# Scaling tokens by two expert weights: the first output tile stored in two transfers of 1 and 11 tokens, and the last tile's weights moved behind the second input tile

## The chip, the core and the metric

The kernel runs on one core of one Trainium2 chip. The metric is the device time of one execution in microseconds; each time given for a kernel is the median of several runs, and one further execution was taken with the hardware profiler. Of the core's engines two compute here: the vector engine (DVE) and the scalar engine (ACT). The sync engine (SP) only issues transfers. All transfers, whichever engine issued them, are carried by the core's 16 DMA engines; the transfers of SP stand in one queue and those of ACT in another.

## The reference: what is computed

Every token is a row of 512 float32 numbers. Each token has two weights, and the output holds the token twice, once times each weight. The expert indices are an input, but nothing is computed from them.

```python
# x (16, 1024, 512) f32, expert_weights (16, 1024, 2) f32
x_expanded = x[:, :, np.newaxis, :].repeat(k, axis=2)     # k = 2
weights = expert_weights[..., np.newaxis]
return (x_expanded * weights).astype(np.float32)          # (16, 1024, 2, 512)
```

So 33.55 MB of tokens and 0.13 MB of weights are read, and 67.11 MB are written.

## The kernel before, in words

**Tiles.** The 16384 tokens are 128 per "token slot" (one in each of the 128 partitions), 128 slots in all. `groups` (line 32) cuts them into six input tiles of 24, 24, 24, 24, 24 and 8 slots; below, "token" means such a slot, as in the title. Within a tile a partition holds consecutive tokens, so that an input tile of 24 is one run of 48 KB in each partition (6144 KB in all). An output tile holds 12 tokens with both copies, which is again 48 KB in each partition; so an input tile gives two output tiles, and the last gives one of 8 tokens. There are 11 output tiles. I number input tiles x0 to x5 and output tiles out0 to out10.

**Buffers.** All weights have one buffer of their own (`w_tile`). Input tiles have two buffers in turn, output tiles two.

**Weights.** SP issues three transfers ahead of everything else: the weights of x0 (line 53, 24 KB, in pieces of 192 bytes), those of x1 to x4 (line 54, 96 KB, in 512 pieces of 192 bytes) and those of x5 (line 58, 8 KB, in 128 pieces of 64 bytes). I call them w0, w-middle and w-last.

**Loads.** `load(i)` (line 74) issues the input tile's transfer on ACT's queue: x0 in six parts of 4 tokens (1024 KB each, 8 KB per partition), every other tile in one. x0 and x1 are issued at the start (line 88), x2 after the instructions of tile 0, and so on (line 119), since the buffer has to be free.

**Compute.** For each token and each of the two weights one multiplication of 128x512 is done, with the weight as a scalar per partition. Counting weights through the whole input as `c`, every third one (`c % 3 == 2`) goes to ACT (line 100) and the two others to DVE (line 106). The first token of x0 has c = 0 and 1, and so both its multiplications are DVE's.

**Stores.** When 12 tokens of an output tile (or the tile's last) are done, SP issues its store (line 115).

**What sets the order.** Each engine works through its own list of instructions in program order; waits between engines are put in by the framework from the tiles' overlaps. A transfer also signals completion on one of eight semaphores, given out in turn; when a semaphore comes round again, the new transfer's issue waits until the earlier transfer on it has landed. In the program before, for instance, the sixth part of x0 waits for w0, and x1 waits for the first part of x0, and out0 waits for w-middle besides its multiplications. Such a wait holds up everything behind it in that engine's list.

Of the kernel before, what the change touches and what calls it, by code (L numbers as in the profile page):

```python
# [1 line left out]

# [4 lines left out]


@with_exitstack
def kernel(  # L10
    ctx: ExitStack,
    tc: tile.TileContext,
    x: bass.AP,
    expert_indices: bass.AP,
    expert_weights: bass.AP,
    out: bass.AP,
):
    nc = tc.nc

    batch, seq, hidden = x.shape  # L20
    k = expert_weights.shape[-1]
    P = nc.NUM_PARTITIONS
    ntok = batch * seq
    assert ntok % P == 0
    A_TOTAL = ntok // P

    f32 = mybir.dt.float32
    row = k * hidden
    TX = 24
    TO = 12  # L30

    groups = [[24], [24], [24], [24], [24], [8]]
    assert sum(sum(g) for g in groups) == A_TOTAL

    xf = x.rearrange("b s h -> (b s) h")
    of = out.rearrange("b s k h -> (b s) (k h)")
    wf = expert_weights.rearrange("b s k -> (b s) k")

    w_pool = ctx.enter_context(tc.tile_pool(name="w_pool", bufs=1))
    x_pool = ctx.enter_context(tc.tile_pool(name="x_pool", bufs=2))  # L40
    o_pool = ctx.enter_context(tc.tile_pool(name="o_pool", bufs=2))

    w_tile = w_pool.tile([P, A_TOTAL * k], f32)

    def rows(of_all, done, T):
        return of_all[done * P : (done + T) * P, :].rearrange(
            "(p a) n -> p (a n)", a=T
        )

    T0 = sum(groups[0])  # L50
    G = len([g for g in groups[1:] if sum(g) == T0])
    head = (1 + G) * T0
    nc.sync.dma_start(out=w_tile[:, : T0 * k], in_=rows(wf, 0, T0))
    nc.sync.dma_start(
        out=w_tile[:, T0 * k : head * k].rearrange("p (g n) -> p g n", g=G),
        in_=wf[T0 * P : head * P, :].rearrange("(g p a) n -> p g (a n)", g=G, p=P),
    )
    nc.sync.dma_start(
        out=w_tile[:, head * k :], in_=rows(wf, head, A_TOTAL - head)
    )  # L60

    tiles = []
    done = 0
    for group in groups:
        T = sum(group)
        a0 = 0
        for n in group:
            tiles.append((done, T, a0, n))
            a0 += n
        done += T  # L70

    loaded = []

    def load(i):
        if i >= len(tiles):
            return
        done, T, a0, n = tiles[i]
        x_tile = x_pool.tile([P, TX * hidden], f32)
        src = rows(xf, done, T)
        step = TX // 6 if i == 0 else n  # L80
        for at in range(0, n, step):
            nc.scalar.dma_start(
                out=x_tile[:, at * hidden : (at + step) * hidden],
                in_=src[:, (a0 + at) * hidden : (a0 + at + step) * hidden],
            )
        loaded.append(x_tile)

    for i in range(2):
        load(i)
    for i, (done, T, a0, n) in enumerate(tiles):  # L90
        x_tile = loaded[i]
        outr = rows(of, done, T)
        for t in range(n):
            if t % TO == 0:
                o_tile = o_pool.tile([P, TO * row], f32)
            for kk in range(k):
                c = (done + a0 + t) * k + kk
                o = t % TO * row + kk * hidden
                if c % 3 == 2:
                    nc.scalar.mul(  # L100
                        out=o_tile[:, o : o + hidden],
                        in_=x_tile[:, t * hidden : (t + 1) * hidden],
                        mul=w_tile[:, c : c + 1],
                    )
                    continue
                nc.vector.tensor_scalar(  # L106
                    out=o_tile[:, o : o + hidden],
                    in0=x_tile[:, t * hidden : (t + 1) * hidden],
                    scalar1=w_tile[:, c : c + 1],
                    scalar2=None,  # L110
                    op0=mybir.AluOpType.mult,
                )
            if (t + 1) % TO == 0 or t + 1 == n:
                at = t // TO * TO
                nc.sync.dma_start(  # L115
                    out=outr[:, (a0 + at) * row : (a0 + t + 1) * row],
                    in_=o_tile[:, : (t + 1 - at) * row],
                )
        load(i + 2)

# [1 line left out]
_INS = ['x', 'expert_indices', 'expert_weights']  # L122
_OUTS = [((16, 1024, 2, 512), 'float32')]


# [23 lines left out]
```

## Time and profile before

| | |
|---|---|
| median of 3 runs | 240.72 us (240.66 to 240.78) |
| profiled execution, its own time | 240.62 us |
| its span, first to last instruction | 238.9 us |
| moved by DMA in the span | 100.81 MB, mean 422 GB/s |
| DVE busy | 69.0 us (29%), 171 multiplications |
| ACT busy | 54.9 us (23%), 85 multiplications and one table load |
| queue of SP (weights and stores) | 2400 packets, 67.24 MB |
| queue of ACT (token loads) | 1584 packets, 33.56 MB |

The profile's page cuts the span into 40 slices of 5.97 us and gives for each the busy tenths of the engines, the mean busy share of the 16 DMA engines, and the GB/s moved. A window view does the same for stretches that one chooses. In both a packet counts, with all its bytes, where it starts; a packet of 48 KB is long (some 1.8 us on its DMA engine), so that the rate in a stretch of a few us can go up and down without any real change. The chain of waits follows the last instruction back to what released it. The list of transfers gives the time from the issue of each to its landing, which holds the time that it stood in the queue.

### The profile page before, as it was taken

How to read it: one execution, taken by the hardware profiler on the slowest of the kernel's cores; microseconds unless marked ns; L12 is line 12 of the kernel's file. 1: busy time of each engine (PE TensorE's matmuls, PEld its weight loads, DVE VectorE, ACT ScalarE, POOL GpSimd, SP SyncE). 2: the span in 40 equal slices, each digit the busy share in tenths (PEclk: the TensorE clock that was granted, in tenths of full speed). 3: DMA queues.
4: the chain of work that ended last, by engine and by line, in shares of the span. 5: the costliest groups of instructions: out<-in, count | busy, mean ns of one | idle time of the engine just before them, and what ended most of it. 6: DMA issues, size and time to landing. Idle time of an engine off the chain costs nothing.

```text
span 238.9 us, 364 instructions
## 1 busy us (share of the span) xinstructions
DVE 69.0 (29%) x171; ACT 54.9 (23%) x86; POOL 0.2 (0%) x4
## 2 busy tenths in 40 slices
DVE  0890300004609100190063037003706406415000
ACT  0870300004308000170071034003406106213000
POOL 0000000000000000000000000000000000000000
DMA  6999999999999999999999999999989899999994
GB/s 244 420 443 395 495 395 395 494 428 395 428 494 395 413 494 411 395 446 469 403 411 502 395 420 453 436 411 428 469 379 496 381 428 469 436 411 428 436 439 197
DMA packets 3986, 100.81 MB, mean 422 GB/s; under 512 B 1168, under 2 KB 1168, under 8 KB 1168
## 3 DMA queue, kind: packets, MB, share of 16 engines
q1 hardware_dynamic: 2400, 67.24, 65.2%
q10 hardware_dynamic: 1584, 33.56, 33.1%
q14 instruction: 2, 0.02, 0.0%
HBM read 33.69 MB, written 67.11 MB: 422 GB/s over the span
## 4 chain that ended last, share of the span: by engine, by line
DMA 66%; DVE 13%; another core or an unknown queue 11%; issue 0%; DVEq 0%; SPq 0%
DMA out_dram<-o_tile 54%; DVE o_tile L106 13%; DMA x_tile<-in_x_dram 11%; DVEq L144 0%; DVEq L106 0%; SPq L115 0%
## 5 line engine op out<-in xcount | busy, mean ns | idle before, releaser
L106 DVE TENSOR_SCALAR o_tile<-x_tile,w_tile 128x512 f32<-128x512 f32 x171 | 69.0, 480 | 149.3 <-DMA out_dram<-o_tile 105.3
L100 ACT ACTIVATE o_tile<-x_tile,w_tile 128x512 f32<-128x512 f32 x85 | 53.6, 709 | 155.5 <-DMA out_dram<-o_tile 116.8
L100 ACT ACT_TABLE_LOAD x1 | 1.3, 1283 | 6.7 <-DMA x_tile<-in_x_dram 6.7
L133 POOL MEMSET const-bfloat16-1.0<- 128x1 bf16 x1 | 0.1, 101 | 0.0
L133 POOL MEMSET const-uint8-127<- 128x1 uint8 x1 | 0.1, 101 | 0.0
L133 POOL MEMSET const-float32-0.0<- 128x1 f32 x1 | 0.1, 98 | 0.2 <-issue 0.2
L133 POOL MEMSET const-float32-1.0<- 128x1 f32 x1 | 0.1, 98 | 0.0
## 6 DMA issues: line engine op xcount, KB each, us to landing
out_dram<-o_tile SPq DMA_DIRECT2D x10, 6144.0 KB, 33.6
x_tile<-in_x_dram ACTq DMA_DIRECT2D x4, 6144.0 KB, 43.9
x_tile<-in_x_dram ACTq DMA_DIRECT2D x6, 1024.0 KB, 10.6
out_dram<-o_tile SPq DMA_DIRECT2D x1, 4096.0 KB, 19.5
x_tile<-in_x_dram ACTq DMA_DIRECT2D x1, 2048.0 KB, 24.0
w_tile<-in_expert_weights_dram SPq DMA_DIRECT2D x1, 96.0 KB, 11.1
w_tile<-in_expert_weights_dram SPq DMA_DIRECT2D x1, 24.0 KB, 2.9
w_tile<-in_expert_weights_dram SPq DMA_DIRECT2D x1, 8.0 KB, 13.2
```

The source lines that it names most:

```text
L100: nc.scalar.mul(out=o_tile[:, o : o + hidden], in_=x_tile[:, t * hidden : (t + 1) * hidden], mul=w_tile[:, c : c + 1],)
L106: nc.vector.tensor_scalar(out=o_tile[:, o : o + hidden], in0=x_tile[:, t * hidden : (t + 1) * hidden], scalar1=w_tile[:, c : c + 1], scala ...
L133: nc = _bacc.Bacc("TRN2", target_bir_lowering=False, num_devices=1)
```

## The change

The order in which the transfers are written down changes, and one store becomes two.

- The weights of the last tile (8 KB) are no longer issued by SP as its third transfer, but by ACT, after x0 and x1, so they stand behind x1 in the queue of loads.
- w-middle is written down after the load of x0; it is still SP's second transfer.
- `cuts` names token 1 as a cut of the first tile, so out0 is stored in two transfers: the first token (512 KB, 4 KB per partition), issued as soon as its two multiplications are done, and the other 11 (5632 KB, 44 KB per partition).

```diff
-    nc.sync.dma_start(out=w_tile[:, : T0 * k], in_=rows(wf, 0, T0))
-    nc.sync.dma_start(
-        out=w_tile[:, T0 * k : head * k].rearrange("p (g n) -> p g n", g=G),
-        in_=wf[T0 * P : head * P, :].rearrange("(g p a) n -> p g (a n)", g=G, p=P),
-    )
-    nc.sync.dma_start(
-        out=w_tile[:, head * k :], in_=rows(wf, head, A_TOTAL - head)
-    )
...
-    for i in range(2):
-        load(i)
+    nc.sync.dma_start(out=w_tile[:, : T0 * k], in_=rows(wf, 0, T0))
+    load(0)
+    nc.sync.dma_start(
+        out=w_tile[:, T0 * k : head * k].rearrange("p (g n) -> p g n", g=G),
+        in_=wf[T0 * P : head * P, :].rearrange("(g p a) n -> p g (a n)", g=G, p=P),
+    )
+    load(1)
+    nc.scalar.dma_start(
+        out=w_tile[:, head * k :], in_=rows(wf, head, A_TOTAL - head)
+    )
+    cuts = [[1]] + [[]] * (len(tiles) - 1)
...
-            if (t + 1) % TO == 0 or t + 1 == n:
-                at = t // TO * TO
+            at = t // TO * TO
+            if t + 1 in cuts[i] or (t + 1) % TO == 0 or t + 1 == n:
+                lo = max([c for c in cuts[i] if c <= t] + [at])
                 nc.sync.dma_start(
-                    out=outr[:, (a0 + at) * row : (a0 + t + 1) * row],
-                    in_=o_tile[:, : (t + 1 - at) * row],
+                    out=outr[:, (a0 + lo) * row : (a0 + t + 1) * row],
+                    in_=o_tile[:, (lo - at) * row : (t + 1 - at) * row],
                 )
```

The semaphores are given out in turn, so the change also moves some of the waits that come from reuse. In the changed program's list ACT issues the six parts of x0, then x1, then w-last, and only then comes its table load and its first multiplication; w-last has the semaphore of w-middle, and its issue waits until w-middle has landed. The first part of the store waits for DVE alone. The second part waits for DVE, for ACT, and for the second part of x0. x2 now waits for the first part of the store where it waited for w-last.

## The prediction

> **What bounds the kernel now.** I read the page's slices first, then the windows, then the chain of waits, then the list of transfers with the starts of the single engines. The slices:
>
> ```profile
> DVE  0890300004609100190063037003706406415000
> ACT  0870300004308000170071034003406106213000
> DMA  6999999999999999999999999999989899999994
> GB/s 244 420 443 395 495 395 395 494 428 395 428 494 395 413 494 411 395 446 469 403 411 502 395 420 453 436 411 428 469 379 496 381 428 469 436 411 428 436 439 197
> ```
>
> The computing engines are idle most of the time, the DMA row is at 9 from the second slice to the last but one, but for two 8s that packets counted at their start explain (the windows below show no loss there). So the kernel is bound by its bytes, and a change can only act where the DMA engines are not full or not at their full rate. The windows (columns: stretch, its length, DVE, ACT, POOL busy with counts, clock, DMA share, GB/s) find those places:
>
> ```profile
> 0.00:2.00 2.00, 0.00 (x0) 0.00 (x0) 0.20 (x4) 1.00 0.19 29
> 2.00:4.00 2.00, 0.00 (x0) 0.00 (x0) 0.00 (x0) 1.00 0.81 299
> 4.00:14.00 10.00, 6.82 (x17) 6.61 (x10) 0.00 (x0) 1.00 1.03 417
> 15.50:16.50 1.00, 0.98 (x3) 0.23 (x1) 0.00 (x0) 1.00 1.07 320
> 16.50:16.90 0.40, 0.40 (x2) 0.40 (x2) 0.00 (x0) 1.00 0.89 225
> 30.00:110.00 80.00, 19.41 (x49) 15.04 (x25) 0.00 (x0) 1.00 1.00 433
> 110.00:220.00 110.00, 36.56 (x91) 28.22 (x45) 0.00 (x0) 1.00 1.00 432
> 236.00:239.00 3.00, 0.00 (x0) 0.00 (x0) 0.00 (x0) 1.00 0.03 11
> ```
>
> From 30 to 220 us the rate is 433 and 432 GB/s, whether loads and stores are mixed or stores run alone. All 100.81 MB at 433 take 232.8 us, so the span of 238.9 holds 6.1 us that are not full rate. I put a price on each place as its length times (1 - rate/433): start 0 to 2 us, 1.9; ramp 2 to 4 us, 0.6; the parts of x0 with the weights between them, 4 to 14 us, 0.4; the dip at 15.5 to 16.9 us, 0.26 + 0.19 = 0.45. That leaves 2.8 us for the end, where the 16 engines finish one after the other and the last signal travels (the last row). The dip lies about two us after out0's store is issued, which is the first store of all:
>
> ```profile
> 13.38 17.16 SPq L115 DMA_DIRECT2D out_dram<-o_tile  x2
> ```
>
> I read the dip as the price of the first stores joining a stream of loads; by 18.7 us the mix runs at its usual rate. A packet counts where it starts, so 0.45 is rough.
>
> The opening as it is issued and as it lands:
>
> ```profile
> 0.73 5.94 ACTq L82 DMA_DIRECT2D x_tile<-in_x_dram  x7
> 5.85 2.46 DVE L106 TENSOR_SCALAR o_tile<-x_tile,w_tile 128x512 f32<-128x512 f32 x6 [5.85 <-DMA x_tile<-in_x_dram]
> 6.70 1.28 ACT L100 ACT_TABLE_LOAD   x1 [6.70 <-DMA x_tile<-in_x_dram]
> 7.99 5.18 ACT L100 ACTIVATE o_tile<-x_tile,w_tile 128x512 f32<-128x512 f32 x8
> ```
>
> ```profile
> w_tile<-in_expert_weights_dram SPq DMA_DIRECT2D x1, 96.0 KB, 11.1
> w_tile<-in_expert_weights_dram SPq DMA_DIRECT2D x1, 24.0 KB, 2.9
> w_tile<-in_expert_weights_dram SPq DMA_DIRECT2D x1, 8.0 KB, 13.2
> ```
>
> The chain of waits says that later on stores follow stores: after each store's landing DVE does 16 multiplications in 6.44 us and the next store is issued, while the other one is still in the queue (6.29 MB at 433 GB/s is 14.5 us even when alone). So the store queue doesn't run dry.
>
> **The change part by part.**
>
> *w-last leaves SP.* w-middle is issued at 1.16 us and lands 11.1 us later, at 12.3: its small pieces go in turn with the 8 KB packets of x0. Before, w-last came behind it (1.63 + 13.2 = 14.8 us). In SP's queue its place is free now.
>
> *w-last in ACT's list.* Its issue waits for w-middle. ACT is in order, so the table load and all of ACT's multiplications wait with it: the table load moves from 6.7 to 12.3 + 0.5 (w-last's issue, the duration that SP showed) = 12.8 us, the first multiplication to 14.1, and the eighth ends at 14.1 + 8 x 0.707 = 19.7 us, where it ended at 13.2. DVE doesn't wait for ACT, and its buffers for out0 and out1 are both free at first. Queued behind ACT are the second part of the store, SP's, and x2, ACT's. The second part is issued at 19.7 us in place of 13.4, which is 6.3 us later. ACT's other eight multiplications of tile 0 are now held by ACT alone: 19.7 + 8 x 0.707 = 25.4 us, where before the last part of x0 let them start only at 28.07 and they ended at 30.1. So out1 and x2 are issued near 25.5, some 4.7 us earlier than 30.2.
>
> On the path this costs nothing as long as the DMA engines have other bytes. They have: x0 and x1 are 2 x 6.29 MB and the first token 0.52 MB, 13.1 MB, which at 417 to 433 GB/s keep them full until about 33 us. If x1 had not been issued at 5.85 us, the 6.3 us would show in full. Then out0's second part and x1 go in turn, out1 is behind in the queue from 25.5 us, and x1 lands earlier than the 57.05 us at which DVE now waits for it. No engine's lateness reaches the store queue after that, by the 14.5 against 6.44 us above. I cost it at 0.
>
> *The first token's store.* DVE's two multiplications end at 5.85 + 2 x 0.48 = 6.8 us. The transfer is issued then, but it stands in SP's queue behind w-middle's pieces, so its bytes move at about 12 us, not at 7. It is 0.52 MB, 1.2 us of all engines, taken from x0: the last parts of x0 come about that much later, and against the present trace the last part is still earlier, since no 48 KB store packets stand between its 8 KB packets until 20 us.
>
> *One more transfer.* It adds 0.33 us on SP's queue, which waits 212 us in all, and 9 more packets on each DMA engine (8 data, 1 signal). Priced by the 0.4 us of 4 to 14 us and the 878 packets under 512 B that start before 14 us, 55 per engine: 0.4 / 55 = 0.007 us each, 0.06 us. w-last's pieces leave that stretch, the same 9 packets, for one where the small price may vanish: between -0.06 and 0. The two together: 0, within 0.06.
>
> The Trainium skill (DMA: Bandwidth & Descriptors, "Anatomy of one DMA" and "Rules for kernel authors") speaks against the cut: it gives each DMA a fixed cost of about 2 us, fitted on another issue path, and wants 1 MiB or more. By that rule, laid end to end, the extra store would make the sum 242.7 us. This trace shows the six 1024 KB parts of x0 following each other in 4 to 14 us at 417 GB/s, so a fixed cost per transfer is hidden while others are queued.
>
> *The joining of stores.* This is the only place where I see a price that changes. Before: one joining, 0.45 us. After: two. The first, at about 12 us, is of 4 KB packets; it ends at about 16 us, and the stores stop. The second, at about 21 us, is of 44 KB packets amid x1's 48 KB loads. Neither is in the trace. For each the lower bound is 0: from 30 us on large loads and stores go in turn without loss, and loads that join running stores show none. The upper bound is the dip, 0.45. So the sum of both is 0 to 0.9 against 0.45, a change of -0.45 to +0.45. I take 0.2 for the first (only 32 KB per DMA engine in all, less to fill the way with) and 0.45 for the second (its packets and its quiet store queue are nearest to the dip's row): +0.2.
>
> *The end.* The last store's size and the last stages are as before. Which of the 16 engines is last can shift; I take 0, within 0.3 of a 2.8 us end.
>
> Sum: 0 + 0 + 0.2 + 0 = +0.2 us. On the profiled execution, 238.9 + 1.7 outside the span = 240.62, that is 240.8; the median of the runs is 0.1 above the profiled execution, so 240.9.
>
> **The rivals.**
>
> *Two full joinings (slower).* If the way has to be filled anew after the stores' pause and small packets cost as much as large ones, the change is +0.45; with the end shifted by up to 0.3 it is 241.2 to 241.5. For it: the dip is there at all, and the stores do pause from about 16 to 21 us. Against it: the dip was seen once, with 8 KB loads.
>
> *Cheaper joining (faster, the other side).* If the small store opens the way under the cover of the 8 KB loads and the large one then joins free like the later mixes, the dip goes: -0.45, with w-last's -0.06 about 240.2. It decides at a saving over 0.48 us, so it needs nearly all of the dip and something of the opening or the end.
>
> *ACT's wait reaches the end (slower).* The 6.3 us in full make 247.0. For it: ACT does stand still until 12.3 us. Against it: 13.1 MB of queued bytes cover 12 us beyond that point. It would need a store queue that runs dry afterwards, and none of the windows from 30 to 220 us shows that.
>
> *The cut doesn't do what it says.* The first token is behind w-middle, so the early store is not early; then the change is nothing but ACT's delay, covered: 240.7. That is inside the forecast's range.
>
> **How the numbers follow.** A difference of 0.2%, 0.48 us, is about what a measurement of this kernel can tell from no change. The forecast with the ineffective cut has 0.53, of which 0.03 crosses the upper bound; two full joinings 0.27, three in ten of it within the bound; the wait reaching the end, in whole or part, 0.04; the cheaper joining 0.16, of which I leave 0.14 beyond the bound. Faster 0.14, slower 0.03 + 0.19 + 0.04 = 0.26, and what is left, 0.60, the same. The range: from 240.72 - 0.45 - 0.06 = 240.2 to 240.72 + 0.45 + 0.06 + 0.3 = 241.5; outside of it are the wait and the tips, under 2 in 10.
>
> **What would show it.** In the changed profile w-middle lands near 12.3 us, ACT's table load starts near 12.8, the second part is issued near 19.7, out1 and x2 near 25.5, and the DMA row stays at 8 or 9 from the second slice on. A window with a reduced rate near 12 to 13 us and another near 20 to 22 tell the joinings: none, one or two. The windows from 50 to 220 us stay at 432 to 433. The prediction is wrong if a slice in the middle is under 8, if the steady rate is another, or if the opening loses a microsecond more or less than here.

## The result: half a per cent slower, and the profile after

The changed kernel's median is 241.93 us (240.82 to 243.43, 21 runs), that of the kernel before in the same comparison 240.72 us (240.55 to 241.4, 21 runs): 1.0051 of the time, with a 95% interval of 1.0041 to 1.0061. That is 1.2 us slower, above the range of 240.2 to 241.5. The spread has grown as well, from 0.85 to 2.6 us. The profiled execution took 241.6 us with a span of 239.8; before it was 240.62 with 238.9.

The slices of the changed kernel's page, as shown of before:

```profile
DMA  7999998999999999999999999999999999999894
GB/s 252 395 417 479 379 503 375 483 410 394 508 410 395 402 492 418 402 460 426 418 451 443 410 443 435 426 410 459 435 404 456 418 465 435 402 443 451 388 437 186
```

Still no slice in the middle is under 8: no stretch went empty. The windows (the same columns as before: stretch, length, DVE, ACT, POOL, clock, DMA share, GB/s):

```profile
4.00:14.00 10.00, 6.60 (x16) 0.81 (x1) 0.00 (x0) 1.00 1.01 397
14.00:30.00 16.00, 6.61 (x16) 10.38 (x17) 0.00 (x0) 1.00 1.02 428
30.00:60.00 30.00, 6.42 (x16) 5.01 (x8) 0.00 (x0) 1.00 1.00 433
60.00:80.00 20.00, 6.42 (x16) 5.02 (x8) 0.00 (x0) 1.00 1.02 433
110.00:220.00 110.00, 36.58 (x91) 28.22 (x45) 0.00 (x0) 1.00 1.00 432
236.00:240.00 4.00, 0.00 (x0) 0.00 (x0) 0.00 (x0) 1.00 0.08 33
```

Two rows of the kernel before beside them:

```profile
14.00:30.00 16.00, 6.25 (x16) 5.00 (x8) 0.00 (x0) 1.00 1.08 444
236.00:240.00 4.00, 0.00 (x0) 0.00 (x0) 0.00 (x0) 1.00 0.03 10
```

The last row is the plainest difference: before, 10 GB/s were left after 236 us, now 33. The window counts a packet where it starts, and that is too coarse for less than a microsecond (it makes 14 to 30 us look slower than before, 428 against 444). So I spread each packet's bytes evenly over its own duration, from the trace's packet records, and took what is missing against 433.3 GB/s:

```
                               before    after
lost up to 40 us                3.78      3.74
lost from 40 to 220 us          0.05      0.59   (0.31 of it in 60 to 80 us)
lost from 220 us to the last
  packet's end                  1.15      1.27
last packet's end             237.64    238.24
from there to the end of span   1.30      1.56
```

The changes add up to -0.04 + 0.54 + 0.12 + 0.26 = 0.88 us, the difference of the two spans. The opening, where the prediction looked, costs nothing more. The loss comes in small pieces later and at the end. The 16 engines' last packets end, before, at 235.8 to 236.7 us on 13 engines and at 237.0, 237.2 and 237.6 on three; after, at 236.2 to 237.1 on 12 engines and at 237.6, 238.1, 238.1 and 238.2 on four.

The opening after the change (timeline rows of the changed kernel: start, duration, engine, line, operation, count, and the wait before it):

```profile
12.82 0.33 ACTq L87 DMA_DIRECT2D w_tile<-in_expert_weights_dram  x1
13.19 1.28 ACT L101 ACT_TABLE_LOAD   x1 [13.19 <-DMA w_tile<-in_expert_weights_dram]
14.48 9.91 ACT L101 ACTIVATE o_tile<-x_tile,w_tile 128x512 f32<-128x512 f32 x16
24.42 0.37 ACTq L74 DMA_DIRECT2D x_tile<-in_x_dram  x1
48.42 5.01 ACT L101 ACTIVATE o_tile<-x_tile,w_tile 128x512 f32<-128x512 f32 x8 [24.03 <-DMA out_dram<-o_tile]
```

ACT stands still until w-middle has landed at 12.8 us, its sixteen multiplications run through without a gap, and x2 is issued at 24.4. The second part of out0 is issued at 19.51 us. At 48.42 ACT waits for a store and no longer for x1, as foretold. The changed kernel's list of transfers (KB, and us from issue to landing):

```profile
out_dram<-o_tile SPq DMA_DIRECT2D x1, 5632.0 KB, 28.8
out_dram<-o_tile SPq DMA_DIRECT2D x1, 512.0 KB, 9.9
w_tile<-in_expert_weights_dram ACTq DMA_DIRECT2D x1, 8.0 KB, 48.2
```

The first token's store, issued at 6.6, lands at 16.5, behind w-middle as said. The last row I had not foreseen. w-last, 8 KB, issued at 12.82, lands at 61 us, and that is not only the wait behind x1, whose packets end at 44.6. Packets by queue in 46 to 60 us (q1: SP's stores, q10: ACT's loads; count, MB, share of 16 engines), first of before:

```profile
q1 hardware_dynamic: 66, 3.24, 53.5%
q10 hardware_dynamic: 67, 2.51, 41.5%
```

and of the changed kernel:

```profile
q1 hardware_dynamic: 133, 5.73, 94.5%
q10 hardware_dynamic: 133, 0.01, 0.6%
```

For 14 us the load queue carries nothing but w-last: 124 packets of 64 bytes and 9 signals of 4 bytes. The store queue has as many packets in that time, 117 of 44 or 48 KB and 16 signals. So each engine takes one packet from each queue in turn, and each 64-byte packet costs the load queue a 48 KB store packet's time. An engine has eight data packets of w-last, 8 x 1.815 = 14.5 us. All that time x2 stands behind them, and its first packets start at about 60 us. I call this the hold. The Trainium skill (DMA: Bandwidth & Descriptors, "Queues, rings and completion order") says that an engine goes round its queues packet by packet, with some 9 to 17 descriptors to a typical packet. The turns here agree, 133 against 133, but not that size: each 64-byte piece took a turn of its own.

### The profile page after: what moved, and what is told of

It is laid out like the page before. It is cut to its first block, busy times and chain, and to the rows that moved or that the text cites. A ratio compares the mean times of both kernels' runs of the same rounds, so it can differ in the third digit from the quotient of the medians.

```text
span 239.8 us, 366 instructions
## 1 busy us (share of the span) xinstructions
DVE 69.1 (29%) x171; ACT 54.5 (23%) x86; POOL 0.2 (0%) x4
## 4 chain that ended last, share of the span: by engine, by line
DMA 75%; DVE 12%; ACT 3%; issue 0%; DVEq 0%; SPq 0%; ACTq 0%
DMA out_dram<-o_tile 70%; DVE o_tile L107 12%; DMA w_tile<-in_expert_weights_dram 5%; ACT o_tile L101 2%; ACT L101 1%; DVEq L146 0%; SPq L80 0%; ACTq L87 0%; DVEq L107 0%; SPq L117 0%
## 6 DMA issues: line engine op xcount, KB each, us to landing
out_dram<-o_tile SPq DMA_DIRECT2D x1, 4096.0 KB, 19.5
```

## The experiments

Each run has its own comparison with the kernel before, whose medians were 240.57 to 240.70 us. "Issued at" is the moment at which SP issues out0's store, or its large part where it is cut.

### The change taken apart

**The cut alone.** w-last goes back to SP as third transfer.

```diff
-    load(1)
-    nc.scalar.dma_start(
+    nc.sync.dma_start(
         out=w_tile[:, head * k :], in_=rows(wf, head, A_TOTAL - head)
     )
+    load(1)
```

> The cut of the first store is kept; the last tile's weights go back to SP's queue, third as before. ACT still has to wait for the middle weights at 12.3 us, now before it issues x1, so ACT starts as late as in the changed kernel. Theory A (the last weights' 8 small packets per DMA engine stand behind x1 and each takes a turn with a 48 KB store packet, 8 x 1.815 = 14.5 us in which the load queue stands still, and what follows from the later loads costs the time): x2 starts right behind x1, no pause, 240.7 within 0.3. Theory B (the joining of the stores twice, that is the cut, costs it): 241.9. Theory C (ACT's late start costs it): 241.9.

Measured: 241.55 us (240.68 to 243.31, 12 runs), ratio 1.0044 [1.0019, 1.0069]. The cut takes one of the eight semaphores more, and now x1's issue waits for w-middle, so ACT is late as in the changed kernel (timeline of this kernel):

```profile
13.65 1.28 ACT L101 ACT_TABLE_LOAD   x1 [13.65 <-DMA w_tile<-in_expert_weights_dram]
24.88 0.36 ACTq L74 DMA_DIRECT2D x_tile<-in_x_dram  x1
```

So this is the cut together with a late large store, without the hold. It costs +1.0. Four of its runs lie at 240.7 to 240.8, like the kernel before, two above 243.

**w-last alone.** The changed kernel without the cut.

```diff
-    cuts = [[1]] + [[]] * (len(tiles) - 1)
+    cuts = [[]] + [[]] * (len(tiles) - 1)
```

> The first store is whole again; the last tile's weights stay behind x1 in the load queue, but their issue waits for the first part of x0 and not for the middle weights, so ACT loses only the issue. Theory A: x1 lands near 57 us as before, then the small packets hold the load queue for 14.5 us until about 70, and the time is 241.9 within 0.5, with a wide spread between runs. Theory B: 240.7. Theory C: 240.7.

Measured: 241.57 us (241.24 to 243.49, 12 runs), ratio 1.0048 [1.0029, 1.0067]. Here ACT is not late: out0 is issued whole at 13.36 us, as before. The hold is there, but short, since out1's packets run out at 62.4. The queues in 57 to 62 us of this kernel:

```profile
q1 hardware_dynamic: 38, 1.57, 72.7%
q10 hardware_dynamic: 69, 0.25, 12.2%
```

In 50 to 70 us this kernel moves 421 GB/s where before moves 433. W-last's new place, the hold with it, costs +1.0 without any cut and without a late store.

**w-last twice.** The changed kernel with a second, unneeded load of the same 8 KB behind w-last (the output is unchanged).

```diff
+    w_more = w_pool.tile([P, (A_TOTAL - head) * k], f32)
+    nc.scalar.dma_start(out=w_more[:, :], in_=rows(wf, head, A_TOTAL - head))
     cuts = [[1]] + [[]] * (len(tiles) - 1)
```

> The changed kernel, with the last tile's weights loaded a second time into a buffer of their own, right behind the first time (8 KB more). Theory A with a price in proportion to the hold: the load queue stands still for 29 us in place of 14.5, x2 starts near 75 us, and the time is 243.1 (twice +1.2). Theory A, but with a price for the loads' being late at all: 241.9 to 242.5. Theories B and C: 241.9.

Measured: 242.68 us (240.33 to 244.04, 12 runs), ratio 1.0058 [1.0028, 1.0088]. The hold is doubled, as the queues in 46 to 74 us show:

```profile
q1 hardware_dynamic: 275, 11.93, 98.5%
q10 hardware_dynamic: 275, 0.02, 0.7%
```

x2's first packets start at 74.5 us. But the time has not moved by a fixed sum: four runs lie at 240.3 to 240.8, no slower than before, and eight at 242.5 to 244.0. In the profiled one 13 engines end at 235.9 to 236.8 and three at 239.3 to 239.5. So a hold of 29 us may cost nothing. In the one slow run that has a profile, three engines are late. (As the runs fall into two groups, the ratio above is not that of the two medians.)

**x2 late in another way.** The kernel before, with x2's load waiting (through a one-element copy on DVE) for the first half of tile 1's work.

```diff
-    def load(i):
+    def load(i, after=None):
...
+        if after is not None:
+            nc.vector.tensor_copy(out=x_tile[:, :1], in_=after)
...
-        load(i + 2)
+            if i == 1 and t + 1 == TO:
+                load(2, after=o_tile[:, t * row : t * row + 1])
+        if i:
+            load(i + 2)
```

> The kernel before, but the load of x2 waits for a one-element copy that DVE makes after the first half of tile 1, so the loads pause for about 10 us between x1 and x2 with no small packets in the queue (the copied element is overwritten by the load). If a pause of the loads by itself costs the time: 241.5 to 242. If it is the small packets between the stores, or the opening: 240.7 within 0.3.

Measured: 245.63 us (245.07 to 246.22, 5 runs), ratio 1.0201 [1.0177, 1.0226]. This answers another question than I had put. While the loads pause, the stores have the engines to themselves, out1 is through at 62.5 us, and the next store is not ready (window of this kernel):

```profile
62.00:65.00 3.00, 2.90 (x9) 0.88 (x2) 0.00 (x0) 1.00 0.27 115
```

The engines stand idle here, since the next store is only issued at 64.12 us, after x1's landing at 57.6 and 6.43 us of DVE. A pause of the loads leaves no gap as long as a store is queued during it, as in the changed kernel; without one it leaves a plain gap.

### The moment of the large store

**The cut with ACT free.** w-last as SP's second transfer, ahead of w-middle, the cut as in the change.

```diff
     nc.sync.dma_start(out=w_tile[:, : T0 * k], in_=rows(wf, 0, T0))
+    nc.sync.dma_start(
+        out=w_tile[:, head * k :], in_=rows(wf, head, A_TOTAL - head)
+    )
     load(0)
...
-    nc.scalar.dma_start(
-        out=w_tile[:, head * k :], in_=rows(wf, head, A_TOTAL - head)
-    )
```

> The cut at token 1 is kept, and the last tile's weights are SP's second transfer, ahead of the middle ones, so that x1 and ACT no longer wait for the middle weights: ACT starts near 7 us. The second part of the store is issued near 13.5 us as the whole one was. If the cut itself (stores that join twice) costs the time: 241.5 with a wide spread. If ACT's late start (the main store 6 us later) costs it: 240.6 within 0.3.

Measured: 249.69 us (248.87 to 250.37, 5 runs), ratio 1.0371 [1.035, 1.0392]. Neither reading expected 9 us. The store was not where I wanted it: its large part waits for w-middle, which lands at 16.6 here, and is issued at 16.72 us. The windows of this kernel:

```profile
30.00:50.00 20.00, 0.00 (x0) 0.00 (x0) 0.00 (x0) 1.00 1.00 395
50.00:70.00 20.00, 6.42 (x16) 5.01 (x8) 0.00 (x0) 1.00 1.01 393
```

The DMA engines are busy all the time, but what they carry goes at 395 and 393 GB/s in place of 433. That speaks against the premise of the prediction that the rate of mixed loads and stores is a fixed thing, and the next runs ask what sets it.

**ACT late, nothing else.** The kernel before, with one tiny multiplication on ACT that reads a weight of w-middle, ahead of its others (the output is unchanged).

```diff
+    early = w_pool.tile([P, 1], f32)
+    nc.scalar.mul(
+        out=early[:, :],
+        in_=w_tile[:, T0 * k : T0 * k + 1],
+        mul=w_tile[:, T0 * k : T0 * k + 1],
+    )
     for i, (done, T, a0, n) in enumerate(tiles):
```

> The kernel before, one store for out0, but ACT's first work is a multiplication of one element per partition that reads a middle weight, so ACT starts at 12.3 us and out0 is issued near 19.5 us in place of 13.4. If ACT's late start costs the time: 241.5 with a wide spread. If the cut itself costs it: 240.6 within 0.3.

Measured: 242.03 us (241.28 to 244.22, 9 runs), ratio 1.0067 [1.0044, 1.009]; out0 is issued at 17.68 us, whole, without cut or hold. A late store, without cut or hold, can cost what the whole change costs.

**The cut in the middle.** The kernel before, with out0 stored in 6 and 6 tokens.

```diff
+    cuts = [[6]] + [[]] * (len(tiles) - 1)
...
```

The store's code behind it is that of the change.

> The kernel before, with out0 stored in two transfers of 6 tokens; the weights as before, ACT on time, both parts issued between 12 and 14 us and so with no pause of the stores between them. If two transfers for out0 are enough to cost the time: 241.5. If it is the pause, or the later main store: 240.6 within 0.3.

Measured: 244.92 us (244.54 to 247.55, 6 runs), ratio 1.0196 [1.0163, 1.0229]. The store's beginning is earlier than before (12.54 us, the second half near 13.5), and the time is worse by 4 us. In the profiled execution, the slowest of them, 130 to 150 us runs at 396 GB/s, and after 236 us there is still much to move (window of this kernel):

```profile
236.00:240.00 4.00, 0.00 (x0) 0.00 (x0) 0.00 (x0) 1.00 0.49 213
```

So a cut without a late store costs too, and more than the one of the change.

**One weight load.** Partition p takes tokens 128 p to 128 p + 127, so that all weights come as one transfer of 1 KB per partition; no cut.

```diff
-    nc.sync.dma_start(out=w_tile[:, : T0 * k], in_=rows(wf, 0, T0))
...
+    nc.sync.dma_start(out=w_tile[:, :], in_=rows(wf, 0, A_TOTAL))
```

> A candidate: partition p holds the tokens p*128 to p*128+127, so that all weights come in one transfer of 1 KB per partition (8 packets per DMA engine in place of 48), and tiles are slices of that; no cut. The opening loses the small packets between the loads of x0, up to 0.3 us: 240.3. If what decides is which DMA engines end late, the new addresses can move it either way: 239.5 to 242.5.

Measured: 242.94 us (241.42 to 244.72, 6 runs), ratio 1.0097 [1.0064, 1.013]. The opening is better (426 GB/s in 4 to 14 us, against 417), the store is earlier (13.04 us), and the kernel is slower. Tokens lie elsewhere in memory in this one, so it says no more than that a cleaner opening is no gain by itself.

**A ladder of moments.** The kernel before with N added multiplications of 128x512 on ACT into a buffer that nobody reads (the output is unchanged). They alternate with out0's own on ACT, so that out0 is issued later. What follows moves too: from N = 2 on x2 is issued at 20.9 to 24.7 us, before at 30.2, and out1 about then as well.

```diff
+    idle = w_pool.tile([P, hidden], f32)
+    for _ in range(N):
+        nc.scalar.mul(
+            out=idle[:, :], in_=loaded[0][:, :hidden], mul=w_tile[:, 2:3]
+        )
     for i, (done, T, a0, n) in enumerate(tiles):
```

N = 2:

> The kernel before with two more multiplications of 128x512 on ACT at the start, into a buffer that nobody reads: out0 is issued 1.4 us later (near 14.8 us), nothing else changes. Theory P (after every start of loads beside stores some DMA engines' 48 KB packets are slow until the engines' turns have settled, and how much that costs depends on the pattern in which they meet, not on how late anything is): anything from 240.3 to 245, and a wider spread than the kernel before. Theory Q (each us by which the main store is late costs, since the ACT-late kernel lost 1.46 us at 4.3 us): 241.0.

Measured: 252.53 us (251.04 to 252.96, 5 runs), ratio 1.048 [1.0458, 1.0502]. The store is issued at 14.13 us, 0.75 us later than before and not the 1.4 that I had reckoned, and that makes 11.8 us, far above what either theory allowed. Windows of this kernel:

```profile
30.00:50.00 20.00, 0.00 (x0) 0.00 (x0) 0.00 (x0) 1.00 1.01 423
50.00:70.00 20.00, 6.43 (x16) 5.01 (x8) 0.00 (x0) 1.00 0.99 420
88.00:94.00 6.00, 4.70 (x12) 3.18 (x6) 0.00 (x0) 1.00 0.78 288
94.00:96.00 2.00, 0.00 (x0) 0.00 (x0) 0.00 (x0) 1.00 0.20 74
137.00:141.00 4.00, 1.71 (x5) 0.19 (x1) 0.00 (x0) 1.00 0.89 320
```

The rate up to 70 us is only some 3% low, and three engines make the difference. By the packet records they are through with out0 at 52.0 to 52.2 us, the other thirteen at 40.5 to 47.9. The buffer of out0 is free when the last engine is through: DVE starts on out2 at 52.88 us. So the next multiplications and the next store come late, and the thirteen engines run dry for 2.2 to 2.9 us each at 91 us, eleven again at 138 to 139. At the end thirteen are done by 243.3 us and three at 248.8 to 249.5. A loss of pace on three engines turns into real gaps on the others.

N = 5:

> As the one with two, but with five more multiplications: out0 is issued 3.5 us later (near 16.9 us). Theory P: anything from 240.3 to 245, not in order with the run of two. Theory Q: 241.8.

Measured: 250.64 us (249.63 to 251.82, 6 runs), ratio 1.0413 [1.0391, 1.0435], with the store at 16.12 us. Windows of this kernel:

```profile
30.00:50.00 20.00, 0.00 (x0) 0.00 (x0) 0.00 (x0) 1.00 0.97 361
50.00:70.00 20.00, 6.42 (x16) 5.01 (x8) 0.00 (x0) 1.00 1.00 371
70.00:90.00 20.00, 1.84 (x5) 1.95 (x4) 0.00 (x0) 1.00 0.99 393
110.00:220.00 110.00, 36.41 (x91) 27.88 (x45) 0.00 (x0) 1.00 1.00 433
```

Here is a loss without any gap: busy engines, slow packets. In 30 to 70 us a 48 KB load packet takes 2.12 us on the mean and one in ten over 2.9, a store packet 2.12 too; in the kernel before both means are 1.82 and the longest load packet is 2.17. From 110 us on all is well.

The control: two added multiplications on tokens from the thirteenth on, behind out0's.

```diff
+            if i == 0 and t == TO:
+                idle = w_pool.tile([P, hidden], f32)
+                for _ in range(2):
+                    nc.scalar.mul(
+                        out=idle[:, :],
+                        in_=x_tile[:, t * hidden : (t + 1) * hidden],
+                        mul=w_tile[:, 2:3],
+                    )
```

> The same two multiplications into a buffer that nobody reads, as in the run that issued out0 later, but on the tokens from the thirteenth on, so behind the eight that out0 needs: out0 is issued at 13.4 us as before, and ACT then has slack until the last part of x0 lands near 28 us. If the moment at which the first store meets the loads is what counts: 240.7 within 0.3. If it is the added instructions or the added buffer: about 252.5.

Measured: 240.79 us (239.84 to 241.61, 12 runs), ratio 1.0002 [0.9987, 1.0017], out0 issued at 13.60. The added instructions cost nothing; the store's moment, with what follows from it, does.

N = 1:

> One multiplication more on ACT ahead of out0's, half of the smallest delay so far, so out0 is issued some 0.1 to 0.7 us later than in the kernel before. If the time goes with the delay in steps of a smooth curve through the kernel before and the run of two (0.75 us, +11.8): up to +11. If it goes by the pattern (theory P): anything from 240.3 to 253, and it need not lie between these two.

Measured: 240.62 us (240.4 to 242.06, 12 runs), ratio 1.0002 [0.9985, 1.002], out0 issued at 13.72. Windows of this kernel:

```profile
30.00:50.00 20.00, 0.00 (x0) 0.00 (x0) 0.00 (x0) 1.00 1.00 433
50.00:70.00 20.00, 6.42 (x16) 5.01 (x8) 0.00 (x0) 1.00 1.00 433
```

The steady rate is there, 0.4 us of issue time away from a kernel that takes 252.5.

N = 8:

> Two queues, eight of the added multiplications among the eight that out0 needs, so out0 is issued near 17.9 us. Zone theory (the time is bad when the first 48 KB stores come in while the DMA engines change from x0's 8 KB to x1's 48 KB packets, about 18 to 21 us, and good ahead of it or behind it): issued at 14.1 and 16.1 it was bad, at 17.7 (ACT waiting for the weights) 242.0, so here 241.5 to 242.5. If more delay by added work is worse, whatever the moment: 250 or more.

Measured: 240.97 us (240.35 to 242.05, 12 runs), ratio 1.0014 [1.0002, 1.0026], out0 issued at 17.86. In 30 to 70 us it runs at 433 again. That is better than the zone theory had it (241.5 to 242.5): behind the bad zone lies a better one.

N = 3:

> Three added multiplications, out0 issued near 14.9 us, between the two bad runs at 14.1 and 16.1. Zone theory: 250 to 253. If the bad runs were accidents of single patterns: anything from 240.5 on.

Measured: 250.54 us (250.2 to 250.96, 4 runs), ratio 1.0411 [1.0394, 1.0428], out0 issued at 14.80; 386 GB/s in 30 to 50 and 381 in 50 to 70 us. It fills the ladder: the zone has no good place between 14.1 and 16.7 that these runs found.

N = 10, meant to bring the store to the changed kernel's own moment:

> The kernel before with ten added multiplications on ScalarE ahead of out0's own (into a buffer that nobody reads; the output is unchanged): out0 should be issued near 19.2 us, whole, w-last stays third on SP, and there is no hold of the load queue. If the time of the changed kernel follows from the moment at which its large store comes in (19.5 us), this gives 241.6 to 242.2 us. If it is the cut or the hold behind the small packets that costs, this gives 240.7 to 241.1 us, as with the store at 17.86 us (240.97).

Measured: 241.46 us (240.94 to 241.79, 7 runs), ratio 1.0035 [1.0021, 1.0049]. It lies between the two forecasts, and it missed the moment. ACT takes one added multiplication for each of its own, so only eight stand ahead of out0's eighth (timeline of this kernel):

```profile
17.24 0.71 ACT L105 ACTIVATE o_tile<-x_tile,w_tile 128x512 f32<-128x512 f32 x1
17.85 0.70 ACT L92 ACTIVATE idle<-x_tile,w_tile 128x512 f32<-128x512 f32 x1
17.97 6.47 SPq L120 DMA_DIRECT2D out_dram<-o_tile  x2
```

The store is issued at 17.97, practically where N = 8 has it; x2 is 1.3 us later (24.10 against 22.76). So it can't tell what the moment of 19.5 costs by itself. But it is a third kernel with a late, whole store and no hold, and it costs +0.8. All rungs in one table, the changed kernel and its two parts among them:

```
out0 (large part)   kernel                           us       ratio
issued at, us
13.36               w-last alone                   241.6      1.0048
13.38               before                         240.7      1
13.60               control                        240.8      1.0002
13.72               N = 1                          240.6      1.0002
14.13               N = 2                          252.5      1.0480
14.80               N = 3                          250.5      1.0411
16.12               N = 5                          250.6      1.0413
16.72               cut with ACT free              249.7      1.0371
17.68               ACT late                       242.0      1.0067
17.86               N = 8                          241.0      1.0014
17.97               N = 10                         241.5      1.0035
19.51               the changed kernel             241.9      1.0051
19.98               the cut alone                  241.6      1.0044
```

The zone of 14.1 to 16.7 lies where the load queue changes from x0's 8 KB packets to x1's 48 KB packets. A store's first large packets start 3.3 to 5 us after its issue. I chained the packet records into 16 engines by their ends and starts, and counted for each engine what of the loads it did around its first large store packet:

```
                     large store    8 KB packets of     packets of x1
                     packets from   x0 behind it        ahead of it      us
before               17.0 us        2 to 4              0              240.7
control              17.2           1 to 3              0              240.8
N = 1                17.4           0 to 3              0              240.6
N = 2                17.8           0 (1 on three)      0 (1 on three) 252.5
N = 3                19.8           0                   1 on all 16    250.5
N = 5                19.8           0                   1 on all 16    250.6
cut with ACT free    21.2           0                   1 (2 on five)  249.7
N = 8                21.4           0                   2 (3 on five)  241.0
N = 10               21.3           0                   2 (3 on four)  241.5
ACT late             21.3           0                   2 (3 on four)  242.0
changed kernel       22.9           0                   2 or 3         241.9
cut alone            24.8           0                   3 on all 16    241.6
```

The orders are those of the one profiled execution, the times medians. The bad kernels are just those in which at least some engines have exactly one packet of x1 ahead of the store. With 8 KB packets still to go, the time in this table is as before; behind two or more, it is 0.3 to 1.5 us longer.

The order shows on single engines too. I added up, for each engine, by how much its packets of 44 and 48 KB up to 60 us were slower than the steady 1.815 us per 48 KB:

```
                     one packet of x1 ahead     otherwise
N = 2                5.4 to 6.6 us on three     0 to 0.4 on thirteen
cut with ACT free    3.2 to 6.2 on eleven       1.3 to 3.6 on five (two ahead)
N = 3 and N = 5      3.8 to 7.2 on all 16       -
N = 8                -                          0.2 to 1.2 on all 16
```

So in N = 2 the three engines that fall behind are the three with one packet ahead. The issue moment of x2, which moves as well, doesn't sort the kernels: 20.9 to 24.7 us in the bad ones, 22.6 to 24.1 in N = 8, N = 10 and ACT late. It is an order that holds in these twelve kernels, not a mechanism, and it doesn't explain everything. The cut alone took 240.71 us in its profiled execution, like the kernel before, and up to 243.3 in others. Four kernels that the table leaves out change something else besides, and with 8 KB packets still to go they are slower all the same: w-last alone +1.0, one weight load +2.4, the cut in the middle +4.3, x2 late +5.1. The change jumps over the bad zone and lands behind it.

### One queue for all

**No cut, loads and stores in SP's queue.** w-last stands behind x1 there.

```diff
-            nc.scalar.dma_start(
+            nc.sync.dma_start(
                 out=x_tile[:, at * hidden : (at + step) * hidden],
...
-    nc.scalar.dma_start(
+    nc.sync.dma_start(
         out=w_tile[:, head * k :], in_=rows(wf, head, A_TOTAL - head)
     )
-    cuts = [[1]] + [[]] * (len(tiles) - 1)
+    cuts = [[]] + [[]] * (len(tiles) - 1)
```

> No cut, the weights in the changed kernel's order, but every load is issued by SP too, so that loads and stores stand in one queue and do not take turns packet by packet. Theory P: no slow packets of 48 KB in the middle and a narrow spread (all runs within 0.5 us); what it may lose is the way's filling at each of some five changes from loads to stores, 0.45 each at most: 240.2 to 242.9. Theory Q says nothing of it.

Measured: 242.82 us (242.67 to 243.16, 4 runs), ratio 1.0091 [1.0078, 1.0104]. The four runs lie closer together than those of any other changed version here, and it is slower: 433 GB/s in 30 to 50 and 428 in 50 to 70 us, and three engines end at 238.1, 239.8 and 239.8 where the others end by 237.4. The Trainium skill (DMA: Bandwidth & Descriptors, "Rules for kernel authors") says that spreading transfers over the issuing engines doesn't help the bandwidth and saves only issue time; here the two queues of the kernel before are 2.1 us better than one, and those of N = 2 are 9.7 us worse. The comparison isn't pure, as the one-queue kernel also has the weights in the changed order.

**One queue with the cut.**

```diff
-    cuts = [[]] + [[]] * (len(tiles) - 1)
+    cuts = [[1]] + [[]] * (len(tiles) - 1)
```

> The changed kernel with all transfers in SP's one queue, the cut at token 1 included. If the cut costs only through the turns that loads and stores take (theory P): the same as the one-queue kernel without the cut, within 0.2. If the extra transfer or the early store costs by itself: 1 us more than that one.

Measured: 243.61 us (243.3 to 244.0, 4 runs), ratio 1.0128 [1.0113, 1.0142]. Theory P, which I held, said no difference from the run above, the other reading 1 us more; it is +0.8. So theory P fails here, and the extra transfer or the early store costs by itself. By the packet records, spread as above, the change from loads to stores in 30 to 34 us runs at 392 and 361 GB/s, without the cut at 420 and 401: 0.3 us of the 0.8. Where the rest goes, and which of the two it is, I can't say.

**One queue, two added multiplications.** This should have told whether the bad zone exists without a second queue.

```diff
+    idle = w_pool.tile([P, hidden], f32)
+    for _ in range(2):
+        nc.scalar.mul(
+            out=idle[:, :], in_=loaded[0][:, :hidden], mul=w_tile[:, 2:3]
+        )
```

> The one-queue kernel with the two multiplications ahead of out0 that cost the two-queue kernel 11.8 us. If that cost comes from loads and stores taking turns packet by packet: 242.8 within 0.3, as the one-queue kernel without them, since the store only stands in line behind x1. If it comes from the delay of the computing engines or the store itself: some us more.

Measured: 242.94 us (242.26 to 243.55, 6 runs), ratio 1.0083 [1.0059, 1.0108]. It tells nothing: out0 is issued at 13.65 us, not later than without the added work (13.87). There ACT waits for tokens of x0 until 11.72 us; the added work goes into that wait, and ACT starts 0.7 us earlier.

## Why the prediction was wrong

- **w-last leaves SP; ACT's wait; the first token's store.** Right to within half a microsecond, x2 to within 1.1: w-middle landed at 12.8 (12.3 said), the table load began at 13.19 (12.8), the second part was issued at 19.51 (19.7), x2 at 24.42 (25.5), and the first token's bytes waited behind w-middle. The rival "the cut doesn't do what it says" was right in this part: the early store is not early.
- **"The joining of stores", +0.2.** Of the right size, and of no weight: two places of lower rate came, somewhat beside the foreseen moments, with 0.39 us more than before at 8 to 12 and 0.38 us at 22 to 28, and the dip of 0.65 us at 16 to 18 went. That is +0.12; with the rest of the opening, 3.74 us against 3.78 up to 40 us. "Two full joinings" (241.2 to 241.5) was the rival nearest in sign and time, but its mechanism is not what cost.
- **"w-last in ACT's list", costed at 0: this step failed.** Its reason was that 13.1 MB of queued bytes cover ACT's wait. They do cover it: between 10 and 220 us no engine stands idle for more than 0.35 us at a time, and the rival "ACT's wait reaches the end" (247.0) is refuted with that. But the cover was the wrong question. Where the first large store comes in among the loads goes with how well the engines carry both afterwards, as the ladder shows. The premise, "from 30 to 220 us the rate is 433 and 432 GB/s, whether loads and stores are mixed or stores run alone", was read off one kernel with its store at 13.38 us, and I took for a property of the chip what goes with that pattern: between 30 and 70 us it is 423 and 420 with the store at 14.13, 361 and 371 at 16.12. Three kernels with a late store and neither cut nor hold (17.68 to 17.97) cost +0.3, +0.8 and +1.5 us; the changed kernel's +1.2 lies among them. (A small reading of the opening was off as well: what ACT issues at 5.85 us is the sixth part of x0, which waits for its first part; x1 waits for w0 and is issued at 6.22.)
- **The same step missed the hold.** I followed w-last's issue through ACT's list and not its packets through the load queue, where they hold back x2 for 14.5 us. By itself, with the store at its old place, w-last's move costs +1.0.
- **"One more transfer", 0 within 0.06: not borne out.** Where the cut is the only difference, in one queue, it costs 0.8 us. How much of that is in the changed kernel no run shows.
- **"The end", 0 within 0.3.** Too tight. Of the 0.88 us by which the span is longer, 0.54 was lost in 40 to 220 us and 0.38 behind 220 us, and single engines carry it to the end: four end 0.5 to 2 us behind the rest.

What stays open is how the 1.2 us divide. The cut with a late store costs 1.0, w-last's move alone 1.0, both together 1.2: they don't add. The cut itself costs something too where the large store's moment hardly changes (one queue +0.8; 6 and 6 tokens +4.3). Each of these seems to set the kernel into another pattern, and the runs of one and the same kernel differ by 2 us and more in several of them. I could not show the moment of 19.5 us alone, nor why an order is slow on the level of the memory or of a DMA engine: the records show that packets take longer, not what they wait for.

No version here beat the kernel before; N = 1 and the control are as fast.

## What to carry to other kernels

A steady rate of mixed loads and stores, read off one profile, holds for that profile: before a change that moves the first large store is costed at nothing because bytes cover it, add a few idle instructions ahead of the store and measure its neighbours, since 0.4 us of issue time can cost 12 us. A small transfer behind large ones in a queue, while another queue carries large packets, costs its queue one large packet's turn for each small packet: here 8 KB held the loads for 14.5 us, and the move cost 1.0 us by itself. And where a kernel is bound by its bytes, look at each DMA engine's last packet: the time is that of the latest engine, not of the mean rate.

## What I had not expected of the hardware

- Engines can be busy 97 to 100% and carry 361 to 371 GB/s: the same 48 KB packets take 2.12 us on the mean in place of 1.82. A bad pattern comes again in every run of its kernel (N = 5: 249.6 to 251.8 in six runs; N = 2: 251.0 to 253.0 in five).
- 64-byte packets go one for one with 48 KB packets of the other queue: with the signals 133 against 133 in 14 us, 275 against 275 in 28 us.
- A slow pattern ends by itself while loads still run: with the store at 16.12 us the rate is 433 GB/s from 110 us on, and the last load ends at 207 us.
- In these kernels the outcome goes by a single packet, engine by engine: with one large load packet ahead of the first large store packet on all or most engines the time is 250 us, with two or three 241 to 242; where only three engines have one ahead (N = 2), those three lose 5.4 to 6.6 us by 60 us and the others at most 0.4.
- A few engines, three or four in most profiles, end 0.3 to 3 us behind the others, the kernel before and the one queue included.
